# A two-block hybrid network in one list-scheduled kernel: new rules and shifts in the scheduler, and an attention score pass over 128 rows in place of 64

## The chip, the cores and the metric

The kernel runs on one core of one Trainium2 chip. The metric is the device time of one launch in microseconds (us), and the time given for a kernel is the median of its runs. The names of the engines are those of the profile: PE is TensorE (PEld is its weight load, which can run beside a product), DVE is VectorE, ACT is ScalarE, POOL is GpSimd, and SP is SyncE, which issues all DMAs here.

## The reference

The input is one sequence of 512 tokens with 1024 channels in float32, and two blocks work on it, one after the other. In short form:

```python
x = first_block(x, c, ...)     # adaptive norm -> gated delta rule (4 heads of 128) beside a short convolution
                               # -> output projection -> adaptive norm -> SwiGLU feed forward -> norm
x = second_block(x, ...)       # norm -> state space scan (16 heads of 64) beside attention (16 heads of 64)
                               # -> two gated branches -> output projection -> norm -> residual

def _forgetting_attention(q, k, v, log_f):          # part of second_block
    fcum = jnp.cumsum(log_f, axis=-1)
    for blk in range(seqlen // ATT_BLOCK):           # 4 blocks of 128 queries
        q0, q1 = blk * ATT_BLOCK, (blk + 1) * ATT_BLOCK
        s = jnp.einsum('bhqd,bhkd->bhqk', q[:, :, q0:q1], k[:, :, :q1]) * scale
        s = s + fcum[:, :, q0:q1, None] - fcum[:, :, None, :q1]
        s = jnp.where(kpos[None, :] <= qpos[:, None], s, -jnp.inf)
        prob = jax.nn.softmax(s, axis=-1)
        outs.append(jnp.einsum('bhqk,bhkd->bhqd', prob, v[:, :, :q1]))
```

## The kernel before

**Products in three passes.** Nearly every matrix product takes each operand apart into a high part of reduced precision (`hi`, type fp32r) and the remainder (`lo`), and adds three products: high by high, high by low and low by high. So every weight block is loaded by a DMA into a tile `raw` (2 buffers), rounded into `hi` by ACT or DVE, and subtracted into `lo` by DVE or POOL (3 buffers each). Activations are pairs in the same way: `h1h`/`h1l` is the normed input of block one, `yh`/`yl` the mixer's output, `h2h`/`h2l` the second norm's, `h3h`/`h3l` the input of block two. A full product has 128 rows to sum over, 128 columns of weights and 512 columns that move through.

**Stages.** A first norm and the modulation (weights `w_ada`, multiplied by the row `crow`: tiles `rawp`, `rawa`) give scale `sc` and shift `sh` of the eight channel tiles k = 0 to 7. The tile `h1h` of each k needs both, and its 24 products follow at once ("first k"). Then come the gated delta rule with its inverses (32 x 32 blocks joined to 64 and 128: sections "join", products `T,N`, `U,Pt`, `Pt,U`) and its scan, the short convolution, the output projection, the feed forward, and in block two the state space scan ("ssd"), the attention in four quarters of four heads ("heads" and "softmax"), the branches and the output.

**Scores.** A head has 64 channels. `qa` holds in rows 0 to 63 the high part of a head's queries and in rows 64 to 127 their low part, and `ka` holds the same 64 rows of keys (high part) twice, so that one product over 128 rows adds two of the three passes. (`qb`, `kb` do this for the pair's other head with the halves exchanged.) The third pass, high queries by low keys, is a product over 64 rows alone: half of `qa` by half of `kl`, which holds the low keys of both heads. There are 4 quarters x 2 pairs x 2 heads x 4 blocks of queries = 64 such second products, 16 each with 512, 384, 256 and 128 columns.

**The order.** The program records its instructions, and `Program.order` puts them into a list schedule, which is then issued engine by engine with the semaphores that the data need. Each instruction has a latest start (`prio`: the PE time ahead of it in program order, plus the `SHIFT` of its section, pulled earlier by what depends on it times `SLACK`). The planner walks forward in time with estimated durations (`price`) and takes the instruction with the smallest `prio` that is ready. An instruction that `also` names a second engine (`tt2`: DVE or POOL; `copy` and `scale`: ACT or DVE) goes to the engine that gets to it first, with `MARGIN` for the second engine. Nothing of the planned time stands in the program that is issued: only the order on each engine is left, and what an instruction waits for. All instructions carry one line number, that of the call in `run` (L224).

Of the kernel before, what the change touches and what calls it, by code (L numbers as in the profile page):

```python
# [23 lines left out]
SLACK = 1.33  # L24
# [4 lines left out]
    "N": -49000, "ab": -120500, "ada": 8500, "branch": 3000, "branch 0": -64500, "branch 0 weights": -64000,  # L29
    "branch 1": 500, "branch 1 weights": 25000, "branch weights": 43500, "conv 0": -4500, "conv 0 weights": -500,  # L30
    "conv 1": 3500, "conv 1 weights": -301500, "decay": -92000, "down 0": -17000, "down 0 weights": 108000,
    "down 2": -13000, "down 2 weights": 62000, "dt": 9000, "ffn 0": -11000, "ffn 0 start": -26500,
    "ffn 0 start weights": 165500, "ffn 0 weights": -110500, "ffn 1": -54000, "ffn 1 weights": 105500,
    "ffn 2": -3000, "ffn 2 weights": -19000, "first 0": -376500, "first 0 weights": -63000, "first 1": 1000,
    "first 1 weights": -1000, "first 2": 3000, "first 2 weights": -21500, "first 3": -27500,
    "first 3 weights": 4500, "first 4": -21500, "first 5": -33000, "first 5 weights": 189500, "first 6": -8000,
    "first 6 weights": -50000, "first 7": 51500, "first 7 weights": -77500, "gate": 500, "gate weights": 43500,
    "h3": 1500, "heads 0 weights": -19500, "heads 1": -89000, "heads 1 weights": 70500, "heads 2": -72500,
    "heads 2 weights": -19500, "heads 3": -1000, "heads 3 weights": 23000, "join 0": -144500, "join 1": 11000,
# [6 lines left out]
    "warm": -42000, "xbc 0 weights": 4000, "xbc 1": 8000, "xbc 1 weights": -1000, "xbc 2": 8000,  # L46
    "xbc 2 weights": 91000, "xbc 3": -69000, "xbc 3 weights": -59500, "y1": 67000, "ys": 135000, "z": 31000,
    "z weights": -73000, "z2 0": -46500, "z2 0 weights": 89500, "z2 1": 500, "z2 1 weights": 41500,
}
MARGIN = {"DVE": 600.0, "ACT": 0.0, "POOL": -500.0}  # L50
# [10 lines left out]
class Program:  # L61
    """Instructions recorded in program order, then issued in the order of a list schedule.

    Dependencies come from the regions that the instructions touch; a tile takes a slot of its
    tag from its first instruction to the end of its last one.
    """
# [45 lines left out]
    def price(self, eng, m, args, kw, out, ins):  # L112
        n = 1
# [4 lines left out]
        if eng == "PE":  # L118
            if m == "transpose":
                return 109.0  # L120
            w = 1
            for d in list(ins[0].shape)[1:]:
                w *= d
            if ins[0].dtype == F32R:
                return max(n * 0.4217, w * 0.836, 20.0)
            return 2 * max(n * 0.836, w * 0.836, 25.0)
# [95 lines left out]
    def run(self, eng, target, m, args, kw, dur):  # L222
        func = str(args[2]).split(".")[-1] if eng == "ACT" else None
        return lambda: getattr(target, m)(*args, **kw), dur, None if func in self.ANY else func  # L224
# [20 lines left out]
    def order(self):  # L245
        ops = self.ops
        # a bank that is not a long sum's is taken once the operands of all its products are there
# [15 lines left out]
        # the latest start of each instruction, were the matrix products issued without a pause  # L263
# [10 lines left out]
        # a tile is free once every instruction that touches it has ended  # L274
# [16 lines left out]
        columns, banks = {}, {}  # L291
        out = []
# [27 lines left out]
        for _ in range(20 * len(ops)):  # L320
# [73 lines left out]
            op.fn, d, f = op.runs[e]  # L394
# [13 lines left out]
            end = s + d  # L408
            if e == "SP":
# [40 lines left out]
def hybrid_kernel(ctx, tc, W, out):  # L450
# [25 lines left out]
    def pg(s, dtype=F32, shape=(P, S)):  # L476
        return tagged("pg", s, shape, dtype)
# [25 lines left out]
    def copy(o, i, scale=None):  # L503
        """o = i * scale, on ScalarE or VectorE"""
# [11 lines left out]
    def tt2(o, i, j, op):  # L516
        """a product or sum of tiles in SBUF, on VectorE or GpSimd"""
# [217 lines left out]
    def ada_first(k):  # L735
        """shift and scale of norm1, channels of k"""
# [126 lines left out]
    # a, beta logits  # L863
# [27 lines left out]
    # per token scalars, [token, chunk, head]  # L891
# [39 lines left out]
    # decay, [j, head, i] per chunk, zero below the diagonal  # L931
# [13 lines left out]
    # token-major keys, scaled  # L945
# [38 lines left out]
    # query norms  # L984
# [15 lines left out]
    # strictly triangular factor and the query-key products  # L1000
# [20 lines left out]
    # inverses of the 32 x 32 diagonal blocks, one block per partition  # L1021
# [39 lines left out]
    # blocks are joined: 32 -> 64 -> 128  # L1061
# [25 lines left out]
    # scan over chunks  # L1087
# [61 lines left out]
    # z gate  # L1149
# [25 lines left out]
    # short convolution branch  # L1175
# [203 lines left out]
    # residual, token-major  # L1379
# [45 lines left out]
    # per token and head: dt, -cumsum(dt a), exp(cumsum), dt exp(sum - cumsum)  # L1425
# [162 lines left out]
    def attention(q):  # L1588
# [13 lines left out]
        for j in range(2):  # L1602
            p_ = psg()
            gemm_T(p_, bk[j], h3, K8)
            ka, kb, kl = pg("ka", F32R), pg("kb", F32R), pg("kl", F32R)
# [4 lines left out]
            tt(kl[0:64], p_[0:64], ka[0:64], op=SUB)  # L1610
# [236 lines left out]
```

## Time and profile before

| What | Value |
|---|---|
| Time, median of 3 runs | 1380.7 us (1377.77 to 1385.73) |
| Span of the profiled execution | 1378.3 us |
| Instructions | 16937 |
| HBM read and written | 144.50 MB and 4.26 MB, 108 GB/s over the span |
| Mean granted TensorE clock | 0.973 of full speed |
| PE groups `h3l,hi`, `h3h,hi`, `h3h,lo` | 448 products each, 165.1, 164.3 and 164.1 us busy |
| ACT table loads | 36, 46.2 us |

The span lies 2.4 us below the median of the runs and within their range. A product's busy time includes its way through the array, so that consecutive products overlap (0.39 us busy for one of 512 columns, of which one starts every 0.23 us); a pace is read from the distance of the starts. "Idle before" is the time in which an engine had nothing running before an instruction, with the instruction that released it.

### The profile page before, as it was taken

The numbers are of one execution on the slowest core, as the hardware profiler recorded it, in microseconds if no ns is written. First come the engines' busy times: TensorE is split into PE (matmuls) and PEld (weight loads), VectorE is DVE, ScalarE is ACT, GpSimd is POOL, SyncE is SP. The second block draws the span as 40 slices with busy tenths as digits, with TensorE's granted clock in tenths as the row PEclk, the third lists the DMA queues.
The fourth block names the chain that finished last, engine by engine and source line by source line (L and its number), as shares of the span: only waits on it lengthen the run. The fifth ranks groups of instructions, "written<-read, shape, count | busy, mean of one in ns | idle before, by whom it ended". The sixth has DMA issues, their size and how long they took to land.

```text
span 1378.3 us, 16937 instructions
## 1 busy us (share of the span) xinstructions
PE 1326.6 (96%) x6403; PEld 1078.6 (78%) x6403; DVE 815.1 (59%) x1502; ACT 591.9 (43%) x1091; POOL 414.3 (30%) x313
## 2 busy tenths in 40 slices
PE   7889998988999999999999999899999999999998
PEld 6567867867988888888878888787788868778887
DVE  7889957876623223332376567974733485865364
ACT  4375245443422123212354546743722464664331
POOL 6635136886211002001273004831200111120141
PEclk8999958989999999999999999999999999999999
DMA  8422133653223222232233223324122324131242
GB/s 295 137 93 92 62 121 124 236 215 117 74 92 120 86 100 92 92 99 87 90 107 142 94 92 109 109 89 92 62 92 92 100 85 118 35 115 54 92 140 105
DMA packets 40660, 149.86 MB, mean 109 GB/s; under 512 B 4097, under 2 KB 12673, under 8 KB 28802
## 3 DMA queue, kind: packets, MB, share of 16 engines
q1 hardware_dynamic: 40578, 148.78, 32.3%
q8 instruction: 50, 0.82, 0.2%
q14 instruction: 32, 0.26, 0.1%
HBM read 144.50 MB, written 4.26 MB: 108 GB/s over the span
## 4 chain that ended last, share of the span: by engine, by line
PE 71%; DVE 4%; ACT 1%; issue 1%; POOL 0%; DVEq 0%; POOLq 0%; ACTq 0%
PE ps L224 71%; DVE tmp L224 1%; DVE lo L224 1%; DVE csb L224 0%; DVE xd L224 0%; DVE z L224 0%; ACT xr L224 0%; DVE prev L224 0%; DVE s L224 0%; POOL lo L224 0%; ACT hi L224 0%; DVE h2l L224 0%; POOL ffl L224 0%; DVE yv L224 0%; ACT z L224 0%
## 5 line engine op out<-in xcount | busy, mean ns | idle before, releaser
L224 ACT ACTIVATE hi<-raw 128x1024 fp32r<-128x1024 f32 (+2 forms) x169 | 173.3, 1029 | 436.8 <-PE ps L224 389.7
L224 DVE TENSOR_TENSOR lo<-raw,hi 128x1024 fp32r<-128x1024 f32 (+2 forms) x168 | 215.6, 1287 | 164.8 <-ACT hi L224 156.5
L224 POOL TENSOR_TENSOR lo<-raw,hi 128x1024 fp32r<-128x1024 f32 (+2 forms) x36 | 84.3, 2341 | 279.2 <-ACT hi L224 193.8
L224 PE MATMUL ps<-h3l,hi 128*128 128x512 f32 x448 | 165.1, 398 | 0.0
L224 PE MATMUL ps<-h3h,hi 128*128 128x512 f32 x448 | 164.3, 396 | 0.0
L224 PE MATMUL ps<-h3h,lo 128*128 128x512 f32 x448 | 164.1, 397 | 0.0
L224 PE MATMUL ps<-h2l,hi 128*128 128x512 f32 (+1 forms) x384 | 135.1, 374 | 2.0 <-DVE h2l L224 2.0
L224 PE MATMUL ps<-h2h,lo 128*128 128x512 f32 (+1 forms) x384 | 134.9, 374 | 1.3 <-DVE lo L224 0.9
L224 PE MATMUL ps<-h2h,hi 128*128 128x512 f32 (+1 forms) x384 | 134.7, 374 | 0.0
L224 POOL TENSOR_TENSOR ffl<-f,ffh 128x512 fp32r<-128x512 f32 x19 | 31.5, 1656 | 247.7 <-ACT ffh L224 247.7
L224 POOL TENSOR_TENSOR rawa<-rawa,crow 128x512 f32<-128x512 f32 x64 | 94.2, 1502 | 31.9 <-DMA rawa<-in_w_ada_dram 31.8
L224 PEld LDWEIGHTS ps<-h3h,lo 128*128 128x128 f32 x448 | 84.0, 188 | 17.6 <-issue 1.3
L224 PEld LDWEIGHTS ps<-h3l,hi 128*128 128x128 f32 x448 | 83.8, 188 | 17.7 <-issue 1.3
L224 PEld LDWEIGHTS ps<-h3h,hi 128*128 128x128 f32 x448 | 83.7, 188 | 17.3 <-issue 1.2
L224 PE MATMUL ps<-h1h,hi 128*128 128x512 f32 x224 | 83.3, 422 | 8.9 <-DVE hi L224 7.0
L224 PE MATMUL ps<-h1h,lo 128*128 128x512 f32 x224 | 82.8, 418 | 5.8 <-DVE lo L224 5.7
L224 PEld LDWEIGHTS ps<-h2l,hi 128*128 128x128 f32 x384 | 72.7, 190 | 14.8 <-DVE h2l L224 2.2
L224 PEld LDWEIGHTS ps<-h2h,lo 128*128 128x128 f32 x384 | 72.7, 190 | 14.7 <-DVE lo L224 1.5
L224 PE MATMUL ps<-h1l,hi 128*128 128x512 f32 x224 | 82.3, 416 | 0.3 <-DVE h1l L224 0.2
L224 PEld LDWEIGHTS ps<-h2h,hi 128*128 128x128 f32 x384 | 72.6, 191 | 12.4
L224 PE MATMUL ps<-ffl,hi 128*128 128x512 f32 x176 | 61.2, 390 | 0.1
L224 PE MATMUL ps<-ffh,hi 128*128 128x512 f32 x176 | 61.2, 389 | 0.0
(438 smaller groups left out, 2747.7 us busy)
## 6 DMA issues: line engine op xcount, KB each, us to landing
raw<-in_w_in_dram SPq DMA_DIRECT2D x38, 1024.0 KB, 4.9
rawa<-in_w_ada_dram SPq DMA_DIRECT2D x39, 512.0 KB, 4.3
raw<-in_w_gate_dram SPq DMA_DIRECT2D x11, 1024.0 KB, 5.0
raw<-in_w_up_dram SPq DMA_DIRECT2D x11, 1024.0 KB, 4.8
raw<-in_w_down_dram SPq DMA_DIRECT2D x8, 1024.0 KB, 4.8
rawp<-in_w_ada_dram SPq DMA_DIRECT2D x18, 256.0 KB, 4.8
raw<-in_w_in_dram SPq DMA_DIRECT2D x8, 512.0 KB, 4.3
raw<-in_w_out_dram SPq DMA_DIRECT2D x4, 1024.0 KB, 5.3
```

What stands on the lines that cost most here:

```text
L224: return lambda: getattr(target, m)(*args, **kw), dur, None if func in self.ANY else func
```

## The change

The change has four parts.

1. **Scores.** The tile `kl` of a pair is split in two: `la` has the low keys of the first head in rows 0 to 63 and zeros in rows 64 to 127, and `lb` has zeros in rows 0 to 63 and the second head's low keys below. The second product of a score then takes the whole of `qa` (or `qb`) and of `la` (or `lb`), over 128 rows. POOL gets 16 memsets of 64 x 512 for it, and the pool `pg` one page more for each pair.
2. **The planner's prices** of a product: 512 columns cost 226.7 ns in the plan where they cost 215.9 ns.
3. **The planner's port rule** (`ports`, `held`): an instruction of DVE with two inputs in SBUF is not planned while a POOL instruction other than a memset runs, and the other way round, and a copy or a product by a scalar within SBUF on DVE is not planned to start while POOL runs anything.
4. **New numbers**: `SLACK`, `MARGIN` and the table `SHIFT`. What can go to two engines is placed anew by this: POOL has 233 instructions where it had 318 (85 fewer, though 16 memsets are new), DVE 1552 where it had 1493, ACT 973 where it had 926; SP's 243 DMAs are the same ones.

```diff
-SLACK = 1.33
+SLACK = 1.26
...
-    "N": -49000, "ab": -120500, "ada": 8500, "branch": 3000, "branch 0": -64500, "branch 0 weights": -64000,
+    "N": -35000, "ab": -206900, "ada": 64700, "blocks": -46500, "branch": -39300, "branch 0": -64300,
...
-MARGIN = {"DVE": 600.0, "ACT": 0.0, "POOL": -500.0}
+MARGIN = {"DVE": 600.0, "ACT": -120.0, "POOL": 360.0}
...
             if ins[0].dtype == F32R:
-                return max(n * 0.4217, w * 0.836, 20.0)
-            return 2 * max(n * 0.836, w * 0.836, 25.0)
+                return max(n * 0.4167 + 13.3, w * 0.836 + 5.0, 25.0)
+            return 2 * max(n * 0.836 + 3.0, w * 0.836 + 5.0, 50.0)
...
+    @staticmethod
+    def ports(eng, m, aps):
+
+        if eng == "POOL":
+            return -1 if m == "memset" else 1
+        if eng != "DVE" or m in ("tensor_reduce", "transpose", "reciprocal", "memset"):
+            return 0
+        n = 1
+        for d in list(aps[0].shape)[1:]:
+            n *= d
+        ins = [a for a in aps[1:] if not (a.shape[-1] == 1 and len(a.shape) == 2 and n > 1)]
+        sb = sum("PSUM" not in str(a.space) for a in ins)
+        if m in ("tensor_scalar", "tensor_copy"):
+            return 2 if sb == 1 and "PSUM" not in str(aps[0].space) else 0
+        return 1 if sb > 1 else 0
...
+            if e in held and op.runs[e][3]:
+                until, other = held["POOL" if e == "DVE" else "DVE"]
+                mine = op.runs[e][3]
+                if until > s and other and (other + mine > 1 or e == "DVE" and mine == 2):
+                    heapq.heappush(fut[e], (until, i))
+                    continue
...
-            ka, kb, kl = pg("ka", F32R), pg("kb", F32R), pg("kl", F32R)
+            ka, kb, la, lb = (pg(n_, F32R) for n_ in ("ka", "kb", "la", "lb"))
+            G.memset(la[64:128].bitcast(F32), 0.0)
+            G.memset(lb[0:64].bitcast(F32), 0.0)
...
-            tt(kl[0:64], p_[0:64], ka[0:64], op=SUB)
-            tt(kl[64:128], p_[64:128], kb[64:128], op=SUB)
-            KS.append((ka, kb, kl))
+            tt(la[0:64], p_[0:64], ka[0:64], op=SUB)
+            tt(lb[64:128], p_[64:128], kb[64:128], op=SUB)
+            KS.append((ka, kb, la, lb))
...
-                    mm(p_[:, :n], QS[j][e][es, bs], KS[j][2][es, :n], start=False, stop=True)
+                    mm(p_[:, :n], QS[j][e][:, bs], KS[j][2 + e][:, :n], start=False, stop=True)
```

The order changes on every engine. Three places follow.

The first is on PE, in the first quarter of the attention, at the scores of a pair's second head (`kb`, `kl` or `lb` by `qb`; the products of `h3` between them are those of the next weight blocks). Before:

```order
L224 MATMUL ps_1602<-h3l_1160,hi_1598 128x512
L224 MATMUL ps_1602<-h3h_1159,lo_1599 128x512
L224 MATMUL ps_1532<-kb_1461,qb_1450 128x512
L224 MATMUL ps_1532<-kl_1462,qb_1450 128x512
L224 MATMUL ps_1513<-pt_1515,vhl_1481 128x512
```

and now:

```order
L226 MATMUL ps_1530<-kb_1461,qb_1450 128x256
L226 MATMUL ps_1532<-kb_1461,qb_1450 128x384
L226 MATMUL ps_1532<-lb_1463,qb_1450 128x384
L226 MATMUL ps_1534<-kb_1461,qb_1450 128x512
L226 MATMUL ps_1534<-lb_1463,qb_1450 128x512
L226 MATMUL ps_1530<-lb_1463,qb_1450 128x256
L226 MATMUL ps_1604<-h3h_1141,hi_1600 128x512
```

The second product of each score stays behind the first one, with `lb` over 128 rows in the place of half of `kl`.

The second place is on PE as well, where the inverses of the delta rule are joined (`T,N`, `U,Pt` and `Pt,U` are the small products of the joins, and the products with `h1` are large ones of other sections). Before:

```order
L224 MATMUL ps_566<-h1h_154,lo_561 128x512
L224 MATMUL ps_400<-U_390,Pt_399 32x32 x4
L224 MATMUL ps_403<-U_390,Pt_402 32x32 x4
L224 MATMUL ps_566<-h1h_162,hi_560 128x512
L224 MATMUL ps_566<-h1l_163,hi_560 128x512
L224 MATMUL ps_566<-h1h_162,lo_561 128x512
L224 MATMUL ps_400<-Pt_399,U_390 32x32 x4
L224 MATMUL ps_403<-Pt_402,U_390 32x32 x4
L224 MATMUL ps_566<-h1h_170,hi_560 128x512
```

and now:

```order
L226 MATMUL ps_400<-U_390,Pt_399 32x32 x4
L226 MATMUL ps_403<-U_390,Pt_402 32x32 x4
L226 MATMUL ps_407<-T_393,N_342 32x32 x3
L226 MATMUL ps_400<-Pt_399,U_390 32x32 x4
L226 MATMUL ps_403<-Pt_402,U_390 32x32 x4
L226 MATMUL ps_407<-T_393,N_342 32x32
L226 MATMUL ps_553<-h1h_202,hi_547 128x512
L226 MATMUL ps_404<-T_391,N_338 64x64 x4
L226 MATMUL ps_409<-U_392,Pt_408 32x32 x4
```

The large products have left the joins: from the first `T,N` to the last `vn,AT` of the scan, 58 of them stood there before, and 19 stand there now, 5 of them within the joins. Small products of the next chunk fill the place.

The third place is on DVE at the start, where the modulation of the channel tiles k is made (`sh` and `sc`; the `rawa` rows are the products with `crow`; `xr` is the normed input of a tile). Before, the second `sh` of the program, that of k = 1, stands behind two of the `rawa` rows:

```order
L224 TENSOR_SCALAR xr_125<-xr_125,sc_107,sh_105 128x512
L224 SCALAR_TENSOR_TENSOR rawa_151,adc<-rawa_151,crow_90 128x1024
L224 SCALAR_TENSOR_TENSOR rawa_159,adc<-rawa_159,crow_90 128x1024
L224 SCALAR_TENSOR_TENSOR sc_107<-adc,bsc_102,colt 128x1
L224 SCALAR_TENSOR_TENSOR sh_105<-adx,colt 128x1
```

and now the end of the stretch that leads to it is this one:

```order
L226 TENSOR_TENSOR lo_166<-raw_64_164,hi_165 128x512 x2
L226 SCALAR_TENSOR_TENSOR rawa_175,adc<-rawa_175,crow_90 128x1024
L226 SCALAR_TENSOR_TENSOR rawa_183,adc<-rawa_183,crow_90 128x1024
L226 SCALAR_TENSOR_TENSOR sc_107<-adc,bsc_102,colt 128x1 x2
L226 TENSOR_TENSOR xr_131<-xT_97,R_33_133 128x512
L226 TENSOR_TENSOR xr_132<-xT_98,R_33_133 128x512
L226 SCALAR_TENSOR_TENSOR rawa_191,adc<-rawa_191,crow_90 128x1024
L226 SCALAR_TENSOR_TENSOR sh_105<-adx,colt 128x1
```

Between the first `xr` (that of k = 0) and the `sh` of k = 1 stood 3 instructions of 128 x 512, 2 of 128 x 1024 and the `sc`; now 12 of 128 x 512 (one of them marked x2), 6 of 128 x 1024 and five `sc` stand there.

More of the change, by code (lines that the diff above doesn't have):

```diff
@@ L28 @@
 SHIFT = {
-    "N": -49000, "ab": -120500, "ada": 8500, "branch": 3000, "branch 0": -64500, "branch 0 weights": -64000,
[L30 to L38, printed above, removed]
@@ L39 @@
-    "heads 2 weights": -19500, "heads 3": -1000, "heads 3 weights": 23000, "join 0": -144500, "join 1": 11000,
[6 rows of a table removed]
-    "warm": -42000, "xbc 0 weights": 4000, "xbc 1": 8000, "xbc 1 weights": -1000, "xbc 2": 8000,
-    "xbc 2 weights": 91000, "xbc 3": -69000, "xbc 3 weights": -59500, "y1": 67000, "ys": 135000, "z": 31000,
-    "z weights": -73000, "z2 0": -46500, "z2 0 weights": 89500, "z2 1": 500, "z2 1 weights": 41500,
+    "N": -35000, "ab": -206900, "ada": 64700, "blocks": -46500, "branch": -39300, "branch 0": -64300,
@@ new lines @@
+    "branch 0 weights": -57000, "branch 1": 1100, "branch 1 weights": 28400, "branch weights": -114900,
+    "conv 0": -6600, "conv 0 weights": -24800, "conv 1": -162600, "conv 1 weights": 2000, "decay": -111700,
+    "down 0": 6200, "down 0 weights": 272300, "down 1": 29400, "down 1 weights": -28100, "down 2": -83900,
+    "down 2 weights": 54300, "dt": 8600, "ffn 0": -400, "ffn 0 start": -41200, "ffn 0 start weights": -8400,
+    "ffn 0 weights": -98300, "ffn 1": -47500, "ffn 1 weights": 359600, "ffn 2": 228900, "ffn 2 weights": -156200,
@@ new lines @@
+    "first 0": -369600, "first 1": -63200, "first 1 weights": -29600, "first 2": 11500, "first 2 weights": -30900,
+    "first 3": -1700, "first 3 weights": 1400, "first 4": 127200, "first 4 weights": -43700, "first 5": -2200,
+    "first 5 weights": 42000, "first 6": -1300, "first 6 weights": 139000, "first 7": 134700,
+    "first 7 weights": -11500, "gate": 9500, "gate weights": 90900, "h3": 22100, "heads 0": -9200,
+    "heads 0 weights": 35300, "heads 1": -95700, "heads 1 weights": 11600, "heads 2": -71900,
@@ L49 @@
+    "heads 2 weights": 91800, "heads 3": -6400, "heads 3 weights": 28900, "inverse": -16100, "join 0": -146800,
[7 rows of a table added]
+    "xbc 0 weights": 153800, "xbc 1": 7300, "xbc 1 weights": 67600, "xbc 2": 3000, "xbc 2 weights": -20000,
+    "xbc 3": -49900, "xbc 3 weights": 56800, "ys": 138400, "z weights": -73000, "z2 0": 400,
+    "z2 0 weights": 272600, "z2 1 weights": 70300,
 }
-MARGIN = {"DVE": 600.0, "ACT": 0.0, "POOL": -500.0}
+MARGIN = {"DVE": 600.0, "ACT": -120.0, "POOL": 360.0}
 COLS = (("b_ada", 48), ("norm1", 8), ("cqkv", 48), ("norm2", 8), ("gdnw", 1), ("csh", 12), ("normf", 8), ("pren", 8),
@@ L223, in run @@
         func = str(args[2]).split(".")[-1] if eng == "ACT" else None
-        return lambda: getattr(target, m)(*args, **kw), dur, None if func in self.ANY else func
+        return (lambda: getattr(target, m)(*args, **kw), dur, None if func in self.ANY else func,
+                self.ports(eng, m, [a for a in list(args) + list(kw.values()) if type(a).__name__ == "AP"]))
+    @staticmethod
[12 more added lines that the diff above has]
+        return 1 if sb > 1 else 0
     def follow(self):
@@ L291, in order @@
         columns, banks = {}, {}
+        held = {"DVE": (0.0, 0), "POOL": (0.0, 0)}
         out = []
@@ L393, in order @@
             op.start = s
-            op.fn, d, f = op.runs[e]
+            op.fn, d, f, port = op.runs[e]
             op.eng = e
@@ L408, in order @@
             end = s + d
+            if e in held:
+                held[e] = end, port
             if e == "SP":
@@ L1637, in attention @@
                 hd = 4 * q + 2 * j + e
-                es = slice(64 * e, 64 * e + 64)
                 nf = pg("nf")
```

13 rows, old and new, of the table SHIFT are left out of this document.

## The prediction

> **What bounds the kernel now.** I read the page's first part (busy time by engine), then its chain of waits, then the windows, since a mean hides stages with different limits.
>
> ```profile
> span 1378.3 us, 16937 instructions
> PE 1326.6 (96%) x6403; PEld 1078.6 (78%) x6403; DVE 815.1 (59%) x1502; ACT 591.9 (43%) x1091; POOL 414.3 (30%) x313
> PE 71%; DVE 4%; ACT 1%; issue 1%; POOL 0%; DVEq 0%; POOLq 0%; ACTq 0%
> ```
>
> The second row says that PE is idle for only 1378.3 - 1326.6 = 51.7 us. The third is the chain that ended last: 71% of the span on it is PE, and no other engine has over 4%. PE is the bound, so time can go in two ways only: PE idles less, or its products start closer together. The windows (start and end, length, then busy time of each engine, the granted TensorE clock, DMA share) show where:
>
> ```profile
> core 0: us, PE busy (x) PEld busy (x) DVE busy (x) ACT busy (x) POOL busy (x), PEclk, DMA share, GB/s
> 0.00:100.00 100.00, 81.76 (x343) 61.36 (x344) 84.10 (x123) 48.00 (x90) 52.70 (x41) 0.92 0.52 181
> 175.00:225.00 50.00, 48.63 (x372) 37.76 (x372) 29.61 (x60) 25.91 (x65) 22.17 (x18) 0.62 0.39 126
> 275.00:375.00 100.00, 88.74 (x510) 76.69 (x509) 70.81 (x91) 42.48 (x77) 58.51 (x38) 0.93 0.39 142
> 375.00:850.00 475.00, 473.62 (x2134) 390.79 (x2133) 204.29 (x241) 169.78 (x236) 88.57 (x59) 1.00 0.29 100
> 850.00:955.00 105.00, 101.32 (x544) 84.89 (x543) 79.25 (x141) 57.73 (x137) 54.78 (x66) 1.00 0.30 92
> 955.00:1250.00 295.00, 293.37 (x1340) 227.43 (x1339) 175.28 (x561) 155.52 (x294) 44.20 (x32) 1.00 0.29 88
> ```
>
> PE idles for 18.2 us in the first 100 and 11.3 us in 275 to 375; in the joins (175 to 225) it is busy at a clock of 0.62. From 955 to 1250, where the attention runs, its idle time is 1.6 us of 295: a new planner can win nothing there, but whatever makes products start closer shortens the span by its full amount, since DVE (175 of 295), ACT (156) and the DMAs (0.29) have room.
>
> **The scores' second pass.** A product's busy time includes its way through the array, so I go by starts. The timeline (start, duration) of the attention gives first two ordinary products, then two places with a second pass:
>
> ```profile
> 1080.18 0.39 PE L224 MATMUL ps<-h3h,lo 128*128 128x512 f32 x1
> 1080.41 0.39 PE L224 MATMUL ps<-h3h,hi 128*128 128x512 f32 x1
> ...
> 987.38 0.39 PE L224 MATMUL ps<-kb,qb 128*128 128x512 f32 x1
> 987.70 0.49 PE L224 MATMUL ps<-kl,qb 64*128 64x512 f32 x1
> 988.12 0.73 PE L224 MATMUL ps<-h3h,hi 128*128 128x512 f32 x2
> 988.70 0.39 PE L224 MATMUL ps<-h3l,hi 128*128 128x512 f32 x1
> ...
> 1238.58 0.40 PE L224 MATMUL ps<-ka,qa 128*128 128x512 f32 x1
> 1238.90 0.49 PE L224 MATMUL ps<-kl,qa 64*128 64x512 f32 x1
> 1239.33 0.33 PE L224 MATMUL ps<-pt,vhl 128*64 128x256 f32 x1
> 1239.50 0.40 PE L224 MATMUL ps<-h3l,hi 128*128 128x512 f32 x1
> ```
>
> An ordinary product of 512 columns takes 0.23 us from start to start (1080.18 to 1080.41). The 64-row product, which has half the rows and the same columns, takes 987.70 to 988.12 = 0.42, so it costs 0.19 more than a full one. The product ahead of it takes 0.32 (0.09 more), and the two behind it take 0.58 in place of 0.46 (0.12 more): 1.32 for four products against 0.92, or 0.40 lost. In the second place it is 0.92 for three products, one of them of 256 columns (half of 0.23): 0.92 - 0.575 = 0.345. Groups by line on the weight loads say the same from the other side:
>
> ```profile
> L224 PEld LDWEIGHTS ps<-kl,qb 64*128 64x128 f32 x32 | 5.8, 183 | 7.7 <-issue 7.2
> L224 PEld LDWEIGHTS ps<-kl,qa 64*128 64x128 f32 x32 | 5.6, 183 | 7.2 <-issue 6.9
> L224 PEld LDWEIGHTS ps<-h3h,hi 128*128 128x128 f32 x448 | 83.7, 188 | 17.3 <-issue 1.2
> ```
>
> The load engine stands idle ahead of a 64-row load for 14.9 / 64 = 0.23 us, ahead of an ordinary one for 17.3 / 448 = 0.04, and what releases it is "issue", no other engine: the load waits until the array is empty. A pass over 128 rows has the shape of its neighbours, so I expect the ordinary pace: it adds zeros, and rows cost nothing in these starts. The loss hangs on the switch and not on the columns, so all 64 passes count: 64 x 0.345 = 22 to 64 x 0.40 = 26, **-24 us** taken. The low bound is the pass's own excess alone, 64 x 0.19 = -12; that the loss stays altogether is a rival.
>
> The Trainium skill, page "TensorEngine Tiling (Array Packing)", speaks both ways. Its Key Properties say that changing the tiling mode drains the engine, which agrees with the 0.23 us idle ahead of these loads and would give the -24. Its section Theoretical Speedup gives up to 2x for a dimension of 64 or less, which speaks against filling the rows with zeros; the 0.42 against 0.23 shows no such gain here, where a 64-row product stands alone between full ones.
>
> **Memsets, pages, DMAs.** Timeline rows of POOL, and the nearest row of a DVE sum over 256 columns:
>
> ```profile
> 37.81 0.36 POOL L224 MEMSET wab<- 128x320 f32 x1
> 43.75 0.96 POOL L224 MEMSET X<- 128x1024 f32 x1 [5.58 <-DVE rawa L224]
> L224 DVE TENSOR_TENSOR yv<-yv,ps 128x256 f32<-128x256 f32 x16 | 6.4, 406 | 1.6 <-PE ps L224 1.6
> ```
>
> A memset of 512 columns lies between 0.36 and 0.96; by its columns about 0.5, 16 of them 8 us (6 to 15) on POOL, which is 30% busy and needed late only for `ffl`. They depend on nothing, so they lie beside PE: 0; were a pair's four buffers late, a score would wait one memset, 8 x 0.96 = 8 us at most. The subtractions into `la` and `lb` are as many and as large as before. SP issues the same 243 DMAs; those reordered move weight blocks by a place or two at a DMA share of 0.29: 0. ACT's five more table loads at 46.2 / 36 = 1.28 are 6.4 us on an engine with 57% to spare: 0.
>
> **The first stage** pays for the order. DVE and PE in the timeline:
>
> ```profile
> 16.94 0.69 DVE L224 TENSOR_TENSOR xr<-xT,ps 128x512 f32<-128x512 f32 x1 [1.97 <-ACT R L224]
> 20.07 1.21 DVE L224 SCALAR_TENSOR_TENSOR rawa<-rawa,crow 128x1024 f32<-128x1024 f32 x1
> 23.45 1.23 DVE L224 SCALAR_TENSOR_TENSOR sc<-adc,bsc,colt 128x1 f32<-128x1 f32 x1
> 24.61 1.29 DVE L224 SCALAR_TENSOR_TENSOR sh<-adx,colt 128x1 f32<-128x1 f32 x1
> 28.66 2.04 PE L224 MATMUL ps<-h1h,hi 128*128 128x512 f32 x4 [4.04 <-DVE hi L224]
> 43.61 0.22 DVE L224 SCALAR_TENSOR_TENSOR sc<-adc,bsc,colt 128x1 f32<-128x1 f32 x1
> 47.66 1.61 PE L224 MATMUL ps<-h1h,hi 128*128 128x512 f32 x6 [1.96 <-DVE hi L224]
> 51.90 0.73 PE L224 MATMUL ps<-h1h,lo 128*128 128x512 f32 x2 [2.63 <-DVE lo L224]
> ```
>
> The same `sc` of one column takes 0.22 at 43.6 and 1.23 at 23.4. POOL is busy for 53 of these 100 us with the products by `crow`, and DVE's instructions with two inputs in SBUF stretch beside it. The stretch before the `sh` of k = 1 (3 of 512 columns, 2 of 1024, one `sc`) is 3 x 0.69 + 2 x 1.21 + 0.22 = 4.7 undisturbed and took 24.61 - 16.94 = 7.7, a factor of 1.6. By the new order it is 13 x 0.69 + 6 x 1.21 + 5 x 0.22 = 17.3 undisturbed: `sh` comes at 34.3 in place of 24.6, or, with the factor, at 45. The port rule is there to keep the factor near 1, so I take 34.3, and PE begins k = 1 nearly 10 us later. Against it, the work of later k that was moved ahead is then done: PE waits 4.0 us at 28.66 now, 2.0 at 47.66 and 2.6 at 51.90, and these 8.6 us can go. Net about **+2**; bounds -5 (the rest of the 18.2 us shrinks too) and +12 (half the stretch factor returns and 8.6 becomes 3).
>
> **The joins.** Large products now stand outside them. Before:
>
> ```profile
> 205.91 0.63 PE L224 MATMUL ps<-h1h,lo 128*128 128x512 f32 x1
> 206.33 0.63 PE L224 MATMUL ps<-h1h,hi 128*128 128x512 f32 x1
> 206.76 1.91 PE L224 MATMUL ps<-vs,U 128*128 128x128 f32 x8
> ...
> 283.58 0.79 PE L224 MATMUL ps<-yh,hi 128*128 128x512 f32 x1 [3.17 <-DVE hi L224]
> 305.94 0.50 PE L224 MATMUL ps<-yh,hi 128*128 128x512 f32 x1 [3.61 <-ACT hi L224]
> ```
>
> Here large products start 0.42 apart, at the halved clock that the 0.62 of the window comes from. Of the 39 that leave (58 to 19), about 34 ran so: run elsewhere at 0.23 they cost 34 x 0.2 = 7 us less. But they filled the time in which a join waits for its copies out of PSUM. Without them such a wait shows; at most it is what the fill took, 34 x 0.43 = 15 us. The bounds are -7 and +8; I take the middle, **0**. The Trainium skill, page "TensorE: Matmul & The Clock Gate", makes the full rate depend on how busy the array has just been; by it bare joins stay slow themselves, and no run here shows yet how large products beside them do.
>
> **Output projection and keys.** At 283.58 and 305.94 PE stands 6.8 us for `hi` of the output projection, most of the 11.3 idle in that window; the new order puts 135 products with `h1` ahead of it, in which these blocks can be made. I take -6 there and -2 for shorter waits at the key branch: **-8**, bounds -13 (all that idle and the latter) and +3.
>
> **The sum**: 1378.3 - 24 + 2 + 0 - 8 = 1348.3 for the span. The median of the runs is 2.4 above the profiled span, so **1350.7 us**. The bounds of the terms together run from -26 - 5 - 7 - 13 = -51 (1330) to -12 + 12 + 8 + 3 = +11 (1392), but all at one end is unlikely: the forecast's own range is 1336 to 1367.
>
> **Rivals.** (a) *The order gives back part of the gain*: first stage +12 and joins +8 at their bad ends, output projection 0, gives 1380.7 - 24 + 20 = 1377. For it: 17 us of DVE ahead of one small `sh`. Against it: the 10 us by which k = 1 comes later are counted in the +2 already. (b) *The order gives more*: terms at good ends, -24 - 5 - 7 - 13 = -49, 1332. For it: 85 fewer POOL instructions beside DVE. (c) *A full-row pass is no faster*: the wait ahead of the load belongs to the score's `qa`, `ka` or its bank, not to the rows; then the first term is 0 and the time 1380.7 - 6 = 1375. Against it: the release is "issue", and the second place has another neighbour with the same loss. Were 64-row products worth half a full one in this kernel, the term would be the rows' price: 64 passes of a mean 320 columns (0.144 us) x one half = +4.6, so 1379. The rule in Theoretical Speedup of the Trainium skill, page "TensorEngine Tiling (Array Packing)", would lead to this. (d) *Slower: DVE becomes the bound* where it is already busy 84, 71 and 79 us (windows 0 to 100, 275 to 375, 850 to 955). About 48 instructions come to it there, 14 + 1 + 3 of 512 columns at 0.69, 4 + 5 of 1024 at 1.22 (the `rawa` row has 1.21) and 6 + 15 of 256 at 0.41: 12.4 + 11.0 + 8.6 = 32 us, 51 with the factor 1.6. If they stand in bunches ahead of `hi` and `lo`, as in the first stage, all of it may fall on PE: 1380.7 - 24 + 51 = 1408. It decides from 24 + 7 = 31 us, 60% of it. Against it: DVE is idle for 16 + 29 + 26 = 71 us in these windows.
>
> **Chances and range.** Forecast 0.61; (a) 0.17; (b) 0.10; (c) 0.06; (d) 0.06. A measurement of this kernel can tell about 0.5% (6.9 us) from no change, so "faster" is below 1373.8 and "slower" above 1387.6. Faster: the forecast, (b), half of (a) and a little of (c), 0.81. Same: the rest of (a) and (c), 0.13. Slower: (d), 0.06. A range of 1332 to 1377 leaves out half of (b), (d), half of (c) and a third of (a), together 0.2.
>
> **What would show it.** Scores: starts 0.23 apart at 512 columns around `la` and `lb`, and "issue" idle ahead of their loads near 0.04; about 24 us less from the first score to the last for the same products, or the first step is wrong. First stage: the start of k = 1 at 35 to 40 and fewer PE waits behind it. Joins: a higher clock in their window. DVE: lower means of `sc`, `lo` and `h1l`. More PE waits on DVE `hi` or `lo` than now would mean (a) or (d).

## The result and the profile after

The changed kernel takes **1333.0 us** (median of 4 runs, 1330.9 to 1334.9) against 1381.5 for the kernel before; the ratio is 0.9652, with a 95% interval of 0.9630 to 0.9674. That is 48.5 us less, where 30 were forecast. The page of the changed kernel has the same rows as before: span, busy time by engine, chain.

```profile
span 1331.9 us, 16908 instructions
PE 1287.0 (97%) x6403; PEld 1071.1 (80%) x6403; DVE 800.4 (60%) x1561; ACT 623.3 (47%) x1138; POOL 250.5 (19%) x228
PE 79%; DVE 11%; ACT 4%; DMA 3%; issue 2%; POOL 1%; SPq 0%; DVEq 0%; POOLq 0%; ACTq 0%
```

Span and idle time of PE give 44.9 us of idle where there were 51.7; the other 40 us were busy time, because products start closer together. DVE has 59 instructions more and is busy for 15 us **less**. The windows of the changed kernel, with the columns of those before (length, busy time by engine, the granted clock of PE, DMA share):

```profile
0.00:100.00 100.00, 78.28 (x336) 61.37 (x337) 75.31 (x130) 48.58 (x107) 28.08 (x31) 0.88 0.51 181
175.00:225.00 50.00, 48.45 (x400) 42.59 (x401) 30.07 (x71) 30.35 (x85) 36.80 (x31) 0.75 0.49 159
275.00:375.00 100.00, 98.15 (x574) 85.87 (x573) 63.03 (x91) 43.96 (x76) 30.61 (x23) 1.00 0.40 143
955.00:1250.00 295.00, 291.50 (x1404) 241.40 (x1404) 171.50 (x468) 157.71 (x282) 20.34 (x28) 1.00 0.30 92
```

From 275 to 375 PE is busy for 98 us of 100 at the full clock (89 and 0.93 before). From 955 to 1250 it does 64 products more in the same time, but now idles for 3.5 us where it idled for 1.6.

Windows at fixed times hold different work in two kernels, so I also sorted the loss by the work that PE has behind it. Each product counts with the lower quartile of the distance of starts of its shape (both kernels together; the 64-row ones as their 128-row fellows); that sums to 1240.3 us of work for either order. What a distance is longer than that is lost, whether PE idles, runs at half the clock or drains. The columns are the stretch of that work in us; the first 50 include the time ahead of the first product, and the 6 us behind the start of the last one are left out:

```
                       0-50  50-100  100-150  150-300  300-850  850-1150  rest    sum
                       first  v and    joins   scan to   feed   attention
                       stage  keys              norm2    forw.,
                                                          ssd
before                 27.7    9.5     14.7     35.1     16.7     27.5     0.5   131.6
scores alone (e1)      30.1    9.5     14.7     37.8     18.7     17.9     0.5   129.2
 POOL's share off (e4) 28.9    4.7     14.3     28.0     19.1     18.5     0.7   114.2
rule alone (e11)       30.3    8.0     13.5     31.7     14.2     10.3     0.6   108.6
changed                33.7    1.4     16.6      9.4     14.0      9.3     0.6    85.0
 64 rows again (e2)    32.5    1.4     15.9      9.4     14.0     24.4     0.6    98.2
 POOL's share back (e3) 36.2   7.1     16.2     15.6     24.7     10.4     0.4   110.7
 rule, MARGIN off (e5) 27.7   14.5     17.3     31.3     20.7     13.8     3.9   129.3
 rule off (e6)         26.5    7.2     17.6     37.2     19.0     13.6     4.0   125.2
 old prices (e7)       29.1    3.1     11.3     29.2     15.6      5.1     0.7    94.2
 old shifts (e8)       30.0    9.9     16.8     13.1     13.6     13.1     0.6    97.1
 rule from 30 us (e9)  26.4    1.4     16.9     14.2     13.8     10.1     0.6    83.3
 POOL free first (e10) 29.7    0.9     19.5     13.7     13.9      7.6     0.6    85.9
 spliced (e12)         28.2    1.4     16.4     10.3     13.6      8.9     0.6    79.5
```

So by these columns the first stage loses 6 more than before, `v` and the keys win 8, the joins lose 2, **the stretch from the scan to the second norm wins 26**, the feed forward and the scan of block two 3, and the attention 18: together 46.6. A column is a fixed stretch of work, and the changed kernel does its joins and its scan earlier in it, so that the border at 150 cuts them at another place. Taken together, from the first `T,N` to the last `vn,AT`, they lose 16.6 us where they lost 25.1, and the way from there to the last sum of the second norm loses 6.5 where it lost 20.5.

Each row is one profiled execution. That of the scores alone is the longest of its four runs (1377.6, median 1371.9) and that of the rule alone the shortest (1357.0, median 1362.4): these two rows differ by 20.6 us where the medians differ by 9.5.

### The profile page after: what moved, and what is told of

The parts are those of the page before. It is cut to its first block, busy times and chain, and to the rows that moved or that the text cites. A ratio compares the mean times of both kernels' runs of the same rounds, so it can differ in the third digit from the quotient of the medians.

```text
span 1331.9 us, 16908 instructions
## 1 busy us (share of the span) xinstructions
PE 1287.0 (97%) x6403; PEld 1071.1 (80%) x6403; DVE 800.4 (60%) x1561; ACT 623.3 (47%) x1138; POOL 250.5 (19%) x228
## 4 chain that ended last, share of the span: by engine, by line
PE 79%; DVE 11%; ACT 4%; DMA 3%; issue 2%; POOL 1%; SPq 0%; DVEq 0%; POOLq 0%; ACTq 0%
PE ps L226 79%; DVE lo L226 2%; DVE s L226 1%; DMA nf<-nfd 1%; ACT hi L226 1%; DVE xr L226 1%; DMA rawa<-in_w_ada_dram 1%; DVE rawa L226 1%; POOL rawa L226 1%; DVE nacc L226 1%; ACT qkv L226 0%; DMA raw<-in_w_in_dram 0%; DVE yl L226 0%; DVE z L226 0%; DMA xT<-in_xT_dram 0%
## 5 line engine op out<-in xcount | busy, mean ns | idle before, releaser
L226 ACT ACTIVATE hi<-raw 128x1024 fp32r<-128x1024 f32 (+2 forms) x185 | 188.5, 1022 | 450.7 <-PE ps L226 386.2
L226 DVE TENSOR_TENSOR lo<-raw,hi 128x1024 fp32r<-128x1024 f32 (+2 forms) x196 | 237.9, 1218 | 197.4 <-ACT hi L226 188.2
L226 PE MATMUL ps<-h3h,lo 128*128 128x512 f32 x448 | 174.8, 396 | 0.0
L226 PE MATMUL ps<-h3l,hi 128*128 128x512 f32 x448 | 174.1, 395 | 0.0
L226 PE MATMUL ps<-h3h,hi 128*128 128x512 f32 x448 | 173.9, 394 | 0.0
L226 PE MATMUL ps<-h2l,hi 128*128 128x512 f32 (+1 forms) x384 | 132.2, 372 | 0.0
L226 PEld LDWEIGHTS ps<-h3h,lo 128*128 128x128 f32 x448 | 84.2, 188 | 16.6
L226 PEld LDWEIGHTS ps<-h3l,hi 128*128 128x128 f32 x448 | 84.2, 188 | 15.9
L226 PE MATMUL ps<-h1h,lo 128*128 128x512 f32 x224 | 79.4, 400 | 3.0 <-DVE lo L226 3.0
L226 PE MATMUL ps<-ffh,lo 128*128 128x512 f32 x176 | 64.4, 389 | 0.0
L226 PE MATMUL ps<-ffl,hi 128*128 128x512 f32 x176 | 64.1, 389 | 0.0
L226 PEld LDWEIGHTS ps<-h1h,hi 128*128 128x128 f32 x224 | 43.3, 195 | 23.0 <-ACT h1h L226 14.0
```

What stands on the lines that cost most here:

```text
L226: return (lambda: getattr(target, m)(*args, **kw), dur, None if func in self.ANY else func, self.ports(eng, m, [a for a in list(args) + li ...
```

## The experiments

Two questions stood open: why the scores' pass did not bring its 24 us and the planner brought about six times the 6 us of its terms. Theory S is the drain of the 64-row pass. Theory P says that POOL's relief (and that of the port) carries the schedule's gain, theory O that it is the place of the products on PE.

**Scores alone, in the kernel before.** The edit is part 1 of the change's diff, nothing else.

> The kernel before with the scores' part of the change alone (la and lb with zeros, 128 rows; old planner, prices and shifts; the old planner places some of the second block anew because of the memsets and the page). Theory S (the 64-row pass drains the array, 0.35 to 0.41 us each): 24 us less than before, 1357 (1352 to 1362). Rival (the wait belongs to the score's operands or bank, rows are indifferent): no change, 1377 to 1385.

Measured: 1371.9 us (1370.1 to 1377.6), ratio 0.9912 (0.9892 to 0.9932): 11 less, half of what S said, and not the rival's 0. As the old planner places other work anew here, the 11 are not the pass by itself; the next run keeps the order.

**64 rows again, in the changed kernel's order.**

The edit is shown in short form: the planner still reckons with the full product, and only the issued product (L1687) has 64 rows.

```diff
-mm(p_[:, :n], QS[j][e][:, bs], KS[j][2 + e][:, :n], start=False, stop=True)
+mm(p_[:, :n], QS[j][e][es, bs], KS[j][2 + e][es, :n], start=False, stop=True)
```

> The changed kernel in its own order, with the second pass over 64 rows again (the zeros are still written, but not read). Theory S: 24 us more than the changed kernel, 1357 (1352 to 1362), and about 0.42 us from the start of such a product to the next at 512 columns. Rival: no change, 1333.

Measured: 1345.8 us (1344.8 to 1346.8), ratio 0.9728 (0.9713 to 0.9744): 13 us more than the changed kernel, again half of what S said. The order is the same, so one place can be laid beside itself. The timeline of the changed kernel, and then that of this run:

```profile
1146.16 0.48 PE L226 MATMUL ps<-ka,qa 128*128 128x512 f32 x1
1146.48 0.39 PE L226 MATMUL ps<-la,qa 128*128 128x512 f32 x1
1146.71 0.40 PE L226 MATMUL ps<-h3h,lo 128*128 128x512 f32 x1
1146.94 0.39 PE L226 MATMUL ps<-h3h,hi 128*128 128x512 f32 x1
```

```profile
1152.73 0.47 PE L226 MATMUL ps<-ka,qa 128*128 128x512 f32 x1
1153.13 0.50 PE L1687 MATMUL ps<-la,qa 64*128 64x512 f32 x1
1153.56 0.50 PE L226 MATMUL ps<-h3h,lo 128*128 128x512 f32 x1
1153.90 0.40 PE L226 MATMUL ps<-h3h,hi 128*128 128x512 f32 x1
```

With zeros the second pass takes 0.23 from start to start and the product behind it 0.23; over 64 rows they take 0.43 and 0.34. Groups by line of the weight loads, first changed, then this run:

```profile
L226 PEld LDWEIGHTS ps<-lb,qb 128*128 128x128 f32 x32 | 6.0, 188 | 1.0
L226 PEld LDWEIGHTS ps<-la,qa 128*128 128x128 f32 x32 | 5.9, 188 | 0.7
```

```profile
L1687 PEld LDWEIGHTS ps<-lb,qb 64*128 64x128 f32 x32 | 5.7, 183 | 7.4 <-issue 7.1
L1687 PEld LDWEIGHTS ps<-la,qa 64*128 64x128 f32 x32 | 5.5, 183 | 6.6 <-issue 6.3
```

The idle time ahead of a load falls from 14.0 / 64 = 0.22 us to 1.7 / 64 = 0.03. Summed over the second passes and their neighbours (by the measure of the table), the loss is 22.8 us before, 21.3 in this run and 1.4 in the changed kernel. **The loss around the 64-row pass is about as large as forecast, and 20 of its 21 us go**; but the time falls by 13 only. The waits of PE in the changed kernel (us in total, times, longest) say where a part of the rest is (the run with 64 rows has no row on `s`):

```profile
PE ps L226 <- ACT h1h L226: 13.4, 2, 11.7
PE ps L226 <- DVE lo L226: 3.9, 3, 3.0
PE ps L226 <- DVE s L226: 3.5, 4, 1.5
```

`s` is a row of the softmax, whose transposes are the next work on PE: with faster scores PE gets there before DVE, and 3.5 us turn into waits; with them the attention loses 4.8 us more outside the second passes than with 64 rows. The remaining 2 us lie in the first stage and the joins, where both runs have the same order and the same products (33.7 and 16.6 us lost against 32.5 and 15.9), and so come from the difference of two executions. In the old order it is the same with larger numbers: the run with the scores alone waits 8.2 us for `s` (DVE 4.9, ACT 3.3), where the kernel before waits 1.6.

**POOL's share put back**, and its mirror: the order that the plan issues is kept, and each instruction that may go to DVE or POOL takes the engine that it has in the other kernel. So each of the two orders was planned for another placement than it runs with, and a part of either result can be that mismatch. (In short form:)

```diff
+plan = prog.order()
+for op, e in zip([op for op in prog.ops if len(op.runs) > 1], TAKE):
+    if e: op.fn = op.runs[e][0]
```

> The changed kernel with each instruction that may go to DVE or POOL on the engine that it had before (114 go back to POOL, 13 to DVE), at its place in the planned order. Theory P (the schedule's gain of some 20 us comes from the relief of POOL and of the port that it shares with DVE): 15 to 25 us more, 1348 to 1358. Theory O (it comes from where the products stand on PE, large ones out of the joins and others ahead of the output projection): 0 to 6 us more, 1333 to 1339.

> The kernel before with the scores over 128 rows and with each instruction that may go to DVE or POOL on the engine that it has in the changed kernel (114 leave POOL), at its place in the old order. Theory P: 15 to 25 us less than the scores' part alone, 1332 to 1342. Theory O: within 6 us of the scores' part alone, 1351 to 1363, or above it where DVE then comes late.

Measured: 1359.5 us (1357.0 to 1360.4) for the first, 26 more than the changed kernel, 1 above the range of theory P; 1367.9 (1362.9 to 1370.0) for the second, only 4 under the scores alone, as theory O has it. Neither holds by itself: the same 127 instructions are worth 26 us in one order and 4 in the other. By the table, their return costs 6 us in the keys, 6 from the scan to norm2, and 11 in the feed forward and ssd. From the scan to norm2, where the changed kernel wins 26, the first run still wins 20 with POOL's share back (15.6 lost), and the second, in the old order, only 7 without it (28.0): there it is the order that brings most of the gain, and less work on POOL the smaller part.

**The planner's parts undone one at a time.** In the changed kernel the port rule and MARGIN were taken out together, then the rule, the prices, and the table of shifts, each by itself:

```diff
-            if e in held and op.runs[e][3]:
+            if False and e in held and op.runs[e][3]:
...
-MARGIN = {"DVE": 600.0, "ACT": -120.0, "POOL": 360.0}
+MARGIN = {"DVE": 600.0, "ACT": 0.0, "POOL": -500.0}
...
-                return max(n * 0.4167 + 13.3, w * 0.836 + 5.0, 25.0)
-            return 2 * max(n * 0.836 + 3.0, w * 0.836 + 5.0, 50.0)
+                return max(n * 0.4217, w * 0.836, 20.0)
+            return 2 * max(n * 0.836, w * 0.836, 25.0)
```

> The changed kernel with the port rule off and the old MARGIN, so that its planner fills POOL again (315 instructions) around the new shifts; 23 large products stand from the joins to the end of the scan (19 in the changed kernel). Theory P (relief of POOL and the shared port): 15 to 27 us more than the changed kernel, 1348 to 1360. Theory O (places of the products): 0 to 6 more, to 1339. In the first 50 us the `sh` of k = 1 stands early on DVE again (place 29 among its instructions, 48 in the changed kernel): the wait of PE for k = 1 is then under 6 us in place of 11.7.

> The changed kernel with only the port rule off (the new MARGIN stays; POOL gets 262 instructions). Theory P: about half of what the run without rule and MARGIN loses, 8 to 14 us more than the changed kernel, 1341 to 1347, most of it where DVE is crowded. Theory O: 1333 to 1337. The `sh` of k = 1 is early again, and the first 50 us lose 4 to 6 us less on PE than in the changed kernel.

> The changed kernel with the old prices of products alone. The planner then puts 162 large products between the first join and the last product of the scan (19 in the changed kernel, 58 before). Theory H (a large product there runs at half the clock and costs 0.2 us more): 143 x 0.2 = 29 us more in that stretch, less the 5 us of waits that they fill, 1350 to 1360. Rival (so many full products keep the granted clock up, and the waits are filled): 1328 to 1336.

> The changed kernel with the old table of shifts (the new SLACK stays): 57 large products stand from the joins to the end of the scan, 8 of them within the joins, and POOL has 238 instructions. Theory O: 10 to 22 us more than the changed kernel, 1343 to 1355, lost between 150 and 330 us. Rival (the rules carry the gain and the shifts are fine tuning): 1333 to 1339.

| Undone | Time, us | Over the changed kernel | Ratio to before |
|---|---|---|---|
| rule and MARGIN (e5) | 1376.7 | 43.7 | 0.9968 (0.9956 to 0.9979) |
| rule (e6) | 1373.8 | 40.7 | 0.9936 (0.9914 to 0.9958) |
| prices (e7) | 1342.6 | 9.6 | 0.9716 (0.9694 to 0.9739) |
| shifts (e8) | 1343.5 | 10.5 | 0.9727 (0.9706 to 0.9747) |

SLACK was not undone by itself. **The port rule is worth three to five times what theory P gave it**; the table of shifts is one that goes with the rule, and no run gave the kernel without the rule a table of its own, so that a part of the 41 us may be a table that no longer fits. The shifts stand at the lower edge of theory O, and the prices between theory H and its rival. With the scores' 13 the single parts add up to 74 us of a total of 48.5: they carry each other. What the rule prevents is seen in the run without it, in the scan and behind it. First PE, then POOL, then DVE in the timeline of that run:

```profile
226.03 2.08 PE L226 MATMUL ps<-vn,AT 128*128 128x128 f32 x8 [5.49 <-DVE vn L226]
256.68 0.80 PE L226 MATMUL ps<-h1h,lo 128*128 128x512 f32 x1 [6.08 <-DVE lo L226]
...
239.60 15.88 POOL L226 TENSOR_TENSOR rawa<-rawa,crow 128x512 f32<-128x512 f32 x10
...
248.45 1.24 DVE L226 SCALAR_TENSOR_TENSOR sc<-adc,bsc,colt 128x1 f32<-128x1 f32 x1
249.61 1.85 DVE L226 SCALAR_TENSOR_TENSOR sca<-sch,colt,sca 128x511 f32<-128x511 f32 x1
251.39 1.22 DVE L226 TENSOR_TENSOR sh<-adc,colt 128x1 f32<-128x1 f32 x1
...
255.41 1.21 DVE L226 TENSOR_TENSOR lo<-raw,hi 128x1024 fp32r<-128x1024 f32 x1
256.55 0.21 DVE L226 SCALAR_TENSOR_TENSOR sc<-adc,bsc,colt 128x1 f32<-128x1 f32 x1
```

POOL multiplies ten times without a pause, 239.6 to 255.5. Beside it a one-column `sc` takes 1.24 us, and 0.21 as soon as POOL is done; the `lo` that PE needs stands at the end of that queue, and PE waits for 6.08 us. The `vn` of the first row is late in the same way: the three instructions on DVE just ahead of it (`sca`, `o`, `sca`) take 1.56 to 1.75 us beside POOL's products. The Trainium skill, page "SBUF — State Buffer", section Who interferes with whom, calls the port pair that DVE and GpSimd share an exclusive lock. The traces agree: of the 32 `sc` and `sh` of one column, 20 take over 0.4 us before, 15 without the rule and 9 in the changed kernel, and each of these ends within 0.02 us of the end of an instruction on POOL (the `sc` above at 249.69, a product of POOL at 249.67), while the others take 0.14 to 0.22. Over the whole kernel the mean of `sc` shows the same (groups by line: before, without the rule, changed):

```profile
L224 DVE SCALAR_TENSOR_TENSOR sc<-adc,bsc,colt 128x1 f32<-128x1 f32 x16 | 12.5, 781 | 3.1 <-ACT rawa L224 3.0
```

```profile
L226 DVE SCALAR_TENSOR_TENSOR sc<-adc,bsc,colt 128x1 f32<-128x1 f32 x16 | 10.8, 682 | 0.9 <-ACT rawa L226 0.9
```

```profile
L226 DVE SCALAR_TENSOR_TENSOR sc<-adc,bsc,colt 128x1 f32<-128x1 f32 x16 | 6.6, 418 | 0.9 <-ACT rawa L226 0.7
```

The run with the old prices settles what I had said of the joins. From the first `T,N` to the last `vn,AT` it has 162 large products and loses 17.5 us, where the changed kernel has 19 and loses 16.6; the run with the old shifts has 57 and loses 18.3. Large products there are **not** dear: theory H falls. What goes with the loss is the rule: in the nine kernels that were planned with it this stretch loses 15.7 to 18.3 us, in the five without it 22.5 to 26.9. The run with the old prices loses its 10 us behind that (17.1 against 3.6 in the work from 250 to 300).

**The rule alone, in the kernel before** (with the scores' part; old prices, MARGIN, shifts).

> The kernel before (old shifts, SLACK, MARGIN and prices) with the scores over 128 rows and with the port rule: POOL gets 249 instructions in place of 321. Theory R (the rule by itself brings most of the schedule's gain): 20 to 30 us less than the scores' part alone (1372), 1342 to 1352. Rival (the gain needs the shifts and prices that go with the rule): 1360 to 1372.

Measured: 1362.4 us (1357.0 to 1363.3), ratio 0.9850 (0.9829 to 0.9872): 9.5 us under the scores alone, by its number the rival. The windows over the scan, first with the scores alone, then with the rule, show that the rule does its work even here:

```profile
202.00:260.00 58.00, 51.73 (x325) 44.43 (x324) 42.84 (x69) 29.25 (x77) 37.43 (x28) 0.82 0.42 138
```

```profile
202.00:260.00 58.00, 58.00 (x369) 50.84 (x368) 46.91 (x74) 31.43 (x79) 37.53 (x26) 0.96 0.45 151
```

PE's 6.3 us of idle go, and the clock rises from 0.82 to 0.96. But later PE stands before the second norm (timeline of the run with the rule, with two ordinary products ahead of the first wait and two behind it):

```profile
313.14 0.28 PE L224 MATMUL ps<-yl,hi 128*128 128x256 f32 x1
313.26 0.28 PE L224 MATMUL ps<-yh,hi 128*128 128x256 f32 x1
...
319.54 0.85 PE L224 MATMUL ps<-ones,nacc 128*128 128x1 f32 x4 [2.88 <-DVE nacc L224]
...
320.82 0.41 PE L224 MATMUL ps<-yl,hi 128*128 128x256 f32 x1
321.04 0.41 PE L224 MATMUL ps<-yh,hi 128*128 128x256 f32 x1
...
328.95 1.01 PE L224 MATMUL ps<-ones,nacc 128*128 128x1 f32 x4 [6.22 <-DVE nacc L224]
```

`nacc` is the sum of squares of norm2, a chain in which PE has hardly any work of its own, and few other products are left to fill it: the filler there is the output projection's products of 256 columns, and 10 of them stand behind the first sum in this run. In the two profiled executions 22 us are won in the scan (150 to 250 of the work) and 16 given back in the norm (250 to 300), a part of them by products of 256 columns that start 0.21 us apart behind the waits and 0.12 ahead of them. The old prices leave little filler too: the changed kernel with them has 17 such products there and loses 17.1 us in 250 to 300. The other twelve kernels have 28 to 33 and lose 2.7 to 7.3.

**The first stage.** PE waits 11.66 us for k = 1 in the changed kernel (PE, then POOL, then DVE in the timeline):

```profile
36.68 1.22 PE L226 MATMUL ps<-h1h,hi 128*128 128x512 f32 x2 [11.66 <-ACT h1h L226]
...
17.18 0.36 POOL L226 MEMSET wab<- 128x320 f32 x1
31.03 0.95 POOL L226 MEMSET X<- 128x1024 f32 x1 [13.50 <-DMA raw<-in_w_in_dram]
31.94 5.04 POOL L226 TENSOR_TENSOR rawp<-rawp,crow 128x512 f32<-128x512 f32 x3
...
34.57 1.21 DVE L226 SCALAR_TENSOR_TENSOR sh<-adx,colt 128x1 f32<-128x1 f32 x1
```

POOL stands for 13.5 us before a memset, and behind that is the `rawp` product which the `sh` of k = 1 needs. (The profile names a DMA; `X` shares its four buffers with `rawa`, and a `rawa` on DVE ends at 30.97, which fits better.) Theory F is that in the plan DVE runs two-input instructions back to back for the first 30 us, so that the rule lets POOL begin none. Two runs loosen the rule there, by `s < 30000.0`, or for POOL's own instructions in the first stage (without the rule altogether, the first 50 us of the work lose 26.5 in place of 33.7):

```diff
-            if e in held and op.runs[e][3]:
+            if e in held and op.runs[e][3] and not (s < 30000.0):
```

> The changed kernel with the port rule off in the first 30 us of the planned time and on behind them. Theory F (at the start the rule holds POOL back behind a DVE that is never idle, so that the second `rawp` product of k = 1 stands behind a memset that waits for a buffer, and `sh` comes 8 us later than it could): the `sh` of k = 1 stands early again (30 among DVE's instructions, 48 in the changed kernel), PE's wait for k = 1 falls from 11.7 us to 5 or less, and the whole is 3 to 9 us faster, 1324 to 1330. Rival (DVE's and POOL's work in the first 80 us sets the end of this stage, and a wait removed at 25 us comes back behind it): 1331 to 1336.

> The changed kernel in which the rule does not hold POOL's own instructions of the first stage (DVE still waits for POOL in the plan). Theory F: PE's wait for k = 1 is 5 us or less, the whole 3 to 9 us faster, 1324 to 1330. Rival: 1331 to 1338.

Measured: 1330.9 us (1326.1 to 1335.7), ratio 0.9628 (0.9595 to 0.9662), and 1339.0 (1334.4 to 1340.8), ratio 0.9684 (0.9663 to 0.9705). In the first of them the long wait is gone and the first 50 us lose 26.4 in place of 33.7, but 5 us come back from the scan to norm2, where its plan places things anew; it cannot be told from the changed kernel, and lies 1 us above the range of theory F. The second is slower and misses both ranges: it loses 4 us less in the first 50, and 3 more in the joins and 4 more behind them. Both plans, the changed one and the one with the rule from 30 us on, issue the same 600 instructions first, in another order; so the last run splices them (in short form: it issues `start`, and then what `rest` has besides).

```diff
+prog.RULE = 30000.0
+start = [(op, op.fn) for op in prog.order()][:600]
+prog.RULE = 0.0
+rest = prog.order()
```

> The plan of the run with the rule off for the first 30 us as far as its 600th instruction, and from there the changed kernel's own order (both plans have issued the same 600 instructions by then). Theory F, with the loss behind it put down to the other plan's later places: the 6 to 8 us saved in the first 50 us stay, 1324 to 1329, faster than the changed kernel by 4 to 9. Rival (a wait saved at the start comes back later whatever the order): 1330 to 1336.

Measured: **1326.8 us** (1324.2 to 1328.1, 5 runs), ratio 0.9599 (0.9577 to 0.9621): 6 under the changed kernel, with no run of the one inside the runs of the other. The first 50 us lose 28.2, the rest as the changed kernel within 1 us a stretch. Theory F holds for the first stage, which loses hardly more than in the kernel before (27.7). That what had come back was the other plan's doing fits too (10.3 us from the scan to norm2 against 14.2), though the runs of the two overlap.

## Why the prediction was right, and where its steps were wrong

The sign was right, and the time (1333.0) lies 1 us inside the range of 1332 to 1377. It lies below the forecast's own 1336 to 1367 and at the sum of rival (b), which had a chance of 0.10, and the parts are others than either's: 11 us too much was forecast for the scores, and some 23 too little for the joins, the scan, the keys and the output projection together. That the total still falls into the range is luck in part.

- **Scores: -24 forecast, -13 measured (-11 in the old order).** The step that failed is "whatever makes products start closer shortens the span by its full amount". The loss around the pass was sized rightly (22.8 us by starts, 1.4 left). The room of DVE and ACT was read from their busy shares, 175 and 156 of 295 us; the softmax is a chain, and a share says nothing of it. The lower bound of -12 held, by another cause than the one it was drawn from.
- **First stage: +2 forecast, +6 measured,** inside the bounds. `sh` was due at 34.3 and came at 34.57, PE began at 36.68 (35 to 40 forecast): adding up DVE's queue was right, though the `rawp` product on POOL, at whose queue I had not looked, left its sum only 0.25 us before that. What failed is "these 8.6 us can go": new waits of 2.4 (for `h1l`, at 41.6) and 3.0 (for `lo`, at 72.4) took their place.
- **Joins: 0 forecast, -8.5 measured** from the first `T,N` to the last `vn,AT`, the stretch of the 58 and 19 large products, and so 1.5 beyond the bound of -7. The price of 0.2 us for each large product was not borne out: with 162 of them the stretch loses 17.5 us, with 19 of them 16.6. The gain goes with the port rule, which the term did not count: PE's waits for the scan's own chain (`vn`, `S`) took 5.1 us before and are gone.
- **Output projection and keys: -8 forecast, bounds -13 and +3.** `v` and the keys gave -8, and the way from the end of the scan to the last sum of norm2 gave -14. This is the term that was mis-sized. The sum counted two waits for `hi` and not the half clock around them (0.93 from 275 to 375 before, 1.00 now), nor that DVE gets faster.
- **Rival (d)**, DVE as the bound, had 32 us of work come to DVE at undisturbed prices. The work came (59 instructions), and DVE's busy time fell from 815 to 800 us, since what already ran there is disturbed less (a mean `sc` takes 0.42 us in place of 0.78). The removal of a neighbour's work was priced as work received only.
- **Rival (c)** is out: "issue" was the drain, since the loss ahead of and behind the pass comes back with its 64 rows and nothing else.

That the rule by itself is worth 41 us in the changed kernel and 9.5 in the old one is measured. That the difference hangs on filler for norm2 is read from the waits, the table and the counts of products there; no run moved that filler alone. The clash on the port is seen in the rows of the run without the rule; how much of the rule's gain is the clash, and how much another effect of the order, stays open, since the kernel with POOL's share back keeps most of the gain from the scan to norm2.

## What to carry to other kernels

Where two engines share a port, count the time that one costs the other: here a planner that keeps their instructions apart took work from POOL, gave it to DVE and still shortened the busy time of both. A busy share shows room only for work that is not part of a chain; after each gain on the bound, look for the next chain (here softmax and norm) and keep independent products to fill it. When parts of a change carry each other, undo them one by one and also add them one by one: the rule was worth 41 us when it was taken out and 9.5 when it was added, and either number alone would mislead.

## What the runs showed of the hardware

A DVE instruction of one column takes 0.14 to 0.22 us alone and up to 1.33 beside POOL's products, longer than one of 1024 columns alone (1.21); the stretched ones end with an instruction of POOL, within 0.02 us. A product over 64 rows among products over 128 takes 0.43 us at 512 columns where a full one takes 0.23, and the product behind it 0.34; filled up with zeros, both take 0.23. In the window from 202 to 260, 6.3 us of idle PE went with a granted clock of 0.82, none with 0.96: a wait costs PE more than its own length, since the products behind it start at half the rate (256 columns 0.21 us apart behind the first wait for `nacc` in the run with the rule alone, 0.12 ahead of it). Small products do not keep the clock up: the window from 175 to 225, which holds most of the joins, has a clock of 0.62 before with PE busy for 97% of it, and of 0.75 in the changed kernel. The Trainium skill, page "TensorE: Matmul & The Clock Gate", Part 1, ties the rate to how busy the array has just been; the clock behind the waits agrees with it.
